# Full-height low parts in the scores of 64-wide heads

## The chip, the cores and the metric

The kernel runs on one core of a Trainium2 chip. The time is the device time of one execution in microseconds (us). The core's engines are named as in the profile: PE (TensorE; PEld is its loading of weights, the stationary operand), DVE (VectorE), ACT (ScalarE), POOL (GpSimd) and SP (SyncE, which here issues the DMAs, in order). Data lie in on-chip memory in 128 partitions; PE multiplies over the partitions, its rows, and accumulates into PSUM.

## What is computed

The reference takes 512 tokens of width 1024 through a gMLP layer, an attention layer with forget gates (FoX) and, in a second block, an mLSTM beside a sparse attention. Each of the first two layers has a SwiGLU FFN. The parts that the change touches are three kinds of score, each a product over heads that are 64 wide:

```python
# FoX, 16 heads of 64
logits = einsum('bhqd,bhkd->bhqk', qi, k) * scale
logits = logits + di[..., :, None] - dcum[..., None, :]
p = softmax(where(kpos <= qpos, logits, -inf))
# indexer of the second block, 8 heads of 64, one key for all heads
sc = relu(einsum('bthd,bsd->bths', iqb, ik))      # then weighted, summed over heads, 128 best keys kept
# sparse attention of the second block, 8 heads of 64: the same scores with a relative bias and the kept keys
```

All is float32. The kernel splits an operand into a high part, rounded to the format that PE multiplies fast, and the low part, the rest, and sums the products of the parts.

## The kernel before

**Large products.** Weights come by SP in chunks of 512 KB (`load_w`, line 271), ACT rounds them to high parts (line 279), DVE or POOL subtracts for the low parts (line 282), and PE runs three matmuls for each pair of tiles (`mm3`, lines 416 to 418): high by high, high by low, low by high, all over 128 rows with 512 columns.

**Scores of 64-wide heads.** A head fills only half of the rows. Therefore `stack` (line 911) lays the queries of a head out over all 128 partitions: the high part on one half, the low part on the other. The keys' high part lies on both halves (`spread`, line 919, does this on the way to DRAM and back), so that one matmul over 128 rows gives high by high and low by high. The third product, queries' high by keys' low, is a second matmul over the 64 rows that hold the queries' high part. It adds to the same PSUM tile:

```python
PE.matmul(sp[:, o:o + w], qs_[:, qs], kh[:, 0:w], start=True, stop=False)        # line 974
PE.matmul(sp[:, o:o + w], qs_[me, qs], kl[me, 0:w], start=False, stop=True)      # line 975
```

`me` is the upper or lower half of the partitions, by the head's number in its pair. The keys' low parts of both heads of a pair share one tile `kl`, a half each. The indexer does the same (lines 1289 and 1290) with one key for all heads, whose high and low parts both lie on both halves already.

**The attentions.** `attention` (line 952) runs over heads. The four tiles of 128 queries are taken in the order SO = (2, 0, 3, 1); tile i has (i + 1) x 128 keys, at least 256 columns. DVE adds the bias and takes the maximum from PSUM (line 980), ACT takes the exponential (982); then come the normalisation, PE's transposes (1001), their splitting by ACT and DVE (1004, 1005) and the product with the values (1016). The scores of a head go ahead of the transposes and values of the head before. Steps of other large products stand between them (`between`, line 507; FILL says how many at which place), so that PE has work while the softmax runs. FoX runs this twice, for 8 heads each, from about 835 to 1000 us; the second block once, from 1567 to 1655 us. The order within each engine is set by a planner that works from the written order and its own costs, but for two stretches that this change doesn't touch.

**The keys' way.** `kdone` (line 1061) splits the keys of a pair of heads and writes them to DRAM, `loader` (line 926) reads the tiles of a pair back while the pair before is worked on. For FoX a pair has three tiles, out of NKB = 6 buffers which the raw keys use before them (`ka`, line 1058). For the second block `ev_a` (line 1265) writes five tiles a pair, two stacks of queries and three of keys, and NQK = 9 buffers hold what is read back. The writes and reads are on SP's queue with all other loads: between the second group of keys and the next product stand, for instance, the eight loads of the layer's input (line 1112), which ACT and DVE turn into `hx` (lines 1113 to 1115).

**The indexer.** Lines 1282 to 1299 go over query tiles 1 to 3 and 8 heads: a pair of matmuls, ACT's relu (1292), DVE's weighted sum (1297). Then DVE searches the 128 best keys (1322, 1323), while PE works on the products that follow.

Of the kernel before, what the change touches and what calls it, by code (L numbers as in the profile page):

```python
"""One-core Trainium2 kernel: a gMLP layer, a FoX attention layer (each with a SwiGLU FFN), then an
mLSTM + indexer-sparse-attention block with a per-layer-embedding gate, for 512 tokens of width 1024.

Large products run as three float32r passes over exactly split operands (hi*hi + hi*lo + lo*hi).
"""
# [30 lines left out]
NKB = 6  # L36
NZ = 26
NQK = 9
# [22 lines left out]
# ------------------------------------------------------------------ host layout  # L61
def _wa(w):
    """[K, N] -> [N/128, 128 (k in tile), K/128 * 128]: stationary chunks of 128 outputs."""
    k, n = w.shape
    return np.ascontiguousarray(
        w.reshape(k // P, P, n // P, P).transpose(2, 1, 0, 3).reshape(n // P, P, (k // P) * P))


def _wb(w):
    """[K, N] -> [N/512, K/256, 128, 2 * 512]: moving chunks of two k tiles by 512 outputs."""  # L70
    k, n = w.shape
    return np.ascontiguousarray(
        w.reshape(k // 256, 2, P, n // 512, 512).transpose(3, 0, 2, 1, 4).reshape(n // 512, k // 256, P, 1024))
# [26 lines left out]
def layout(i):  # L100
# [33 lines left out]
    # gMLP  # L134
# [14 lines left out]
    # FoX  # L149
# [8 lines left out]
    # second block  # L158
# [3 lines left out]
    # rows of the last tile: keys 0-63, input gates 64-67, forget gates 96-99, indexer weights 100-107  # L162
# [28 lines left out]
# ------------------------------------------------------------------ kernel body  # L191
def body(tc, nc, a):
    V, S_, G, PE = nc.vector, nc.scalar, nc.gpsimd, nc.tensor

    with ExitStack() as es:
# [55 lines left out]
        # ---------------- constants  # L251
# [14 lines left out]
        # ---------------- weights: load, split  # L266
# [7 lines left out]
        def wsplit(src, n=1024, share=0, alloc=None, raw=None):  # L274
            """share: every share-th low part on GpSimd"""
# [9 lines left out]
        # ---------------- modulation vectors, worked off between weight chunks  # L285
# [21 lines left out]
        def fill(n=1):  # L307
            """one column's load, and the product for the one loaded before"""
# [25 lines left out]
        def gain(csc, gname):  # L334
            """gain * (1 + scale), a column per feature tile"""
# [5 lines left out]
        def gb_row(cg, gname):  # L341
            """gate * gain, on every partition"""
# [13 lines left out]
        # ---------------- norms, transposes  # L356
        def rsq(out, ss, scale):
            """out = 1 / sqrt(ss * scale + eps)"""
# [3 lines left out]
        def norm_rows(xr, out):  # L362
            """out = xr / rms(xr), a token tile in two halves"""
# [8 lines left out]
        def to_T(ts, xn, g, sh, hi, lo, js=range(KD), spill=None):  # L372
            """token-major halves of the tiles ts -> feature-major hi, lo; what is transposed goes
            to spill as well"""
# [39 lines left out]
        # ---------------- products  # L414
# [5 lines left out]
        def gemm_a(h, w, n, evac, m=P, group=0, nfill=0, share=0, gshare=1):  # L420
            """out^T tile i (m outputs by 512 tokens), weights stationary. The first group goes by
            halves of the tokens, since the second half of h comes later."""
# [20 lines left out]
        def gemm_b(h, w, groups, kt, evac, head=False, tail=0, nfill=0, share=0, raws=(), hshare=1):  # L443
            """out tile (g, t): 128 tokens by 512 outputs, activations stationary. The last chunks
            of a group (all of them in the first with head) go token tile by token tile."""
# [25 lines left out]
        def chunks_a(h, w, n, evac):  # L471
            """gemm_a's weight chunks for between(): source, number of steps, step"""
# [15 lines left out]
        def chunks_b(h, w, g, kt, evac):  # L488
            """gemm_b's weight chunks of a group for between()"""
# [17 lines left out]
        def between(chunks, share=1):  # L507
            """products to be placed between the steps of something else: a function that emits the
            next n steps (all that are left without n)"""
# [24 lines left out]
        def post(gb, xsrc, xdst, alloc, done):  # L534
            """x += gate * rms_norm(y), then x / rms(x) by token tiles"""
# [23 lines left out]
        def halves(h, g, sh, spill=None):  # L559
            """takes normalised token tiles; transposes two at a time"""  # L560
# [33 lines left out]
        # ================= layer 0: gMLP  # L594
# [5 lines left out]
        with tc.tile_pool(name="l0", bufs=20) as p0:  # L600
# [8 lines left out]
            # loads in the order of their use: per-layer embedding, x, modulation with weights  # L609
# [16 lines left out]
            # relative bias by distance 511 - m  # L626
# [26 lines left out]
            def norm2(t):  # L653
                """two token tiles"""
# [14 lines left out]
            with tc.manual_schedule(engines={mybir.EngineType.Activation, mybir.EngineType.DVE, mybir.EngineType.PE, mybir.EngineType.SP}):  # L669
                S_.activation(crow, crow, AF.Silu)  # L670
                # brings in the table of the square root
# [31 lines left out]
                # the first products start as the modulation of each feature tile is there  # L703
# [50 lines left out]
                # both gains and the scale of the attention's scores, for the keys  # L754
# [40 lines left out]
            def ready(g):  # L795
                """the spatial weights of a group of features, and its values normalised"""
# [46 lines left out]
        # ================= FFN 0  # L843
# [10 lines left out]
        # ================= layer 1: FoX attention  # L854
        cmask = const("cmask", [P, P], "mask")
        def headnorm(out, alloc, done=None):
            """rms norm of heads of 64, token-major; one square root for a group of token tiles"""
# [21 lines left out]
        def vsplit(g, t, pt, alloc, done):  # L879
            """values of 8 heads -> tiles of 4 heads; a pair of heads as hi lo lo hi"""  # L880
# [9 lines left out]
        def logsig(out, xin, n, tmpa):  # L890
            """min(x, 0) - ln(1 + exp(-|x|))"""
# [13 lines left out]
        def pt_tiles(pool, bufs=1):  # L905
            """transposed probabilities, hi and lo: the blocks of key tile s from PTO[s] on"""
# [4 lines left out]
        def stack(src, alloc):  # L911
            """two heads, feature-major: hi over lo for the first, lo over hi for the second"""
# [6 lines left out]
        def spread(d, q0, hi, lo):  # L919
            """two heads' keys to DRAM: hi of each on both halves of the partitions, and their lo"""  # L920
# [131 lines left out]
        with tc.tile_pool(name="x", bufs=1) as px:  # L1052
# [116 lines left out]
            def fprep(pr):  # L1169
                return *stack(pair_t(qt_, pr), qk), *kload(pr)  # L1170
# [446 lines left out]
```

## Time and profile before

| what | value |
|---|---|
| median of 3 runs | 1938.3 us (1936.7, 1938.3, 1945.61) |
| the profiled execution | 1936.7 us, with a span of 1936.7 us |
| PE busy | 1880.1 us, 97% of the span |
| weight loads (PEld), beside PE | 1523.1 us |
| DVE, ACT, POOL busy | 1123.1, 794.6, 375.8 us |
| chain that ended last | PE 78%, DVE 11%, DMA 7% |

A busy PE isn't a PE at its peak: matmuls overlap, and each counts from its start to its modelled end. How fast PE really goes is read from the starts of successive matmuls in the order of time. The granted clock is a share: 1.00 is 2.4 GHz, 0.50 is 1.2 GHz. Idle time of an engine other than the slowest costs nothing by itself; it matters who waits for that engine.

### The profile page before, as it was taken

What the parts mean: (1) busy time and instruction counts of PE and PEld (TensorE: products, weight loads), DVE (VectorE), ACT (ScalarE), POOL (GpSimd) and SP (SyncE); (2) the same over time, 40 slices, a digit from 0 to 9 for tenths busy, and PEclk for the clock granted to TensorE, in tenths of its full rate; (3) what the DMA queues carried; (4) which work ended last, traced back from release to release, by engine and by line L of the source; (5) the groups of instructions that cost most, each with busy time, mean ns of one, the idle gap of its engine ahead of it and who ended that gap; (6) DMA issues with size and microseconds to landing.
All of it is one profiled execution on the core that took longest, in us unless ns stands there. A gap on an engine that the chain in (4) does not pass through costs nothing.

```text
span 1936.7 us, 23791 instructions
## 1 busy us (share of the span) xinstructions
PE 1880.1 (97%) x8688; PEld 1523.1 (79%) x8688; DVE 1123.1 (58%) x2132; ACT 794.6 (41%) x1395; POOL 375.8 (19%) x216
## 2 busy tenths in 40 slices
PE   7999998999999999999998999999989999999998
PEld 5788877888878877877777888888876877888887
DVE  7879735677762275367757333322365967856534
ACT  5334324422231255477655222222344246455334
POOL 2100123222220013433322111100020353022011
PEclk9999999999999999999998999999987999999999
DMA  8674753477763446733512322233243633322522
GB/s 330 235 274 137 251 194 109 147 265 260 260 219 109 141 138 205 247 120 126 172 67 97 112 94 96 98 109 126 103 136 98 187 129 111 115 93 88 191 96 100
DMA packets 106191, 299.46 MB, mean 155 GB/s; under 512 B 11893, under 2 KB 14749, under 8 KB 106074
## 3 DMA queue, kind: packets, MB, share of 16 engines
q1 hardware_dynamic: 106074, 297.94, 45.3%
q8 instruction: 69, 1.13, 0.2%
q14 instruction: 48, 0.39, 0.1%
HBM read 266.35 MB, written 34.16 MB: 155 GB/s over the span
## 4 chain that ended last, share of the span: by engine, by line
PE 78%; DVE 11%; DMA 7%; issue 2%; ACT 2%; POOL 0%; SPq 0%; DVEq 0%; ACTq 0%
PE acc L416 22%; PE acc L418 22%; PE acc L417 22%; DMA raw<-in_ada 6%; DVE raw L302 3%; PE tp L975 2%; PE tp L1016 2%; DVE d L302 1%; PE tp L1001 1%; PE tp L974 1%; DVE h L408 1%; PE tp L384 1%; DVE wlo L282 1%; DVE h L409 1%; PE tp L815 1%
## 5 line engine op out<-in xcount | busy, mean ns | idle before, releaser
L279 ACT ACTIVATE whi<-raw 128x1024 fp32r<-128x1024 f32 x293 | 309.9, 1059 | 679.4 <-PE acc L418 305.5
L282 POOL TENSOR_TENSOR wlo<-raw,whi 128x1024 fp32r<-128x1024 f32 x124 | 305.1, 2464 | 1368.3 <-ACT whi L279 1189.1
L417 PE MATMUL acc<-h,whi 128*128 128x512 f32 (+1 forms) x1112 | 418.2, 376 | 10.5 <-DVE h L409 10.4
L416 PE MATMUL acc<-h,whi 128*128 128x512 f32 (+1 forms) x1112 | 418.6, 376 | 5.5 <-DVE h L408 5.2
L418 PE MATMUL acc<-h,wlo 128*128 128x512 f32 (+1 forms) x1112 | 417.5, 375 | 3.3 <-DVE wlo L282 2.7
L282 DVE TENSOR_TENSOR wlo<-raw,whi 128x1024 fp32r<-128x1024 f32 x169 | 212.4, 1259 | 312.6 <-ACT whi L279 312.2
L417 PEld LDWEIGHTS acc<-h,whi 128*128 128x128 f32 x1112 | 212.5, 191 | 48.6 <-DVE h L409 12.7
L416 PE MATMUL acc<-whi,h 128*128 128x512 f32 x608 | 242.5, 399 | 7.9 <-DVE h L408 6.5
L416 PEld LDWEIGHTS acc<-h,whi 128*128 128x128 f32 x1112 | 212.8, 191 | 43.2 <-DVE h L408 6.0
L418 PEld LDWEIGHTS acc<-h,wlo 128*128 128x128 f32 x1112 | 212.7, 191 | 41.9 <-DVE wlo L282 4.5
L417 PE MATMUL acc<-wlo,h 128*128 128x512 f32 x608 | 240.0, 395 | 3.2 <-DVE wlo L282 3.2
L418 PE MATMUL acc<-whi,h 128*128 128x512 f32 x608 | 240.8, 397 | 0.0
L302 DVE SCALAR_TENSOR_TENSOR raw<-raw,cact 128x1024 f32<-128x1024 f32 x96 | 148.9, 1562 | 75.4 <-DMA raw<-in_ada 69.8
L416 PE MATMUL acc<-whi,s 128*128 128x512 f32 (+1 forms) x488 | 190.4, 390 | 0.7 <-DVE t L1308 0.7
L417 PE MATMUL acc<-wlo,s 128*128 128x512 f32 (+1 forms) x488 | 190.7, 391 | 0.0
L418 PE MATMUL acc<-whi,s 128*128 128x512 f32 (+1 forms) x488 | 190.2, 390 | 0.0
L416 PEld LDWEIGHTS acc<-whi,h 128*128 128x128 f32 x608 | 115.5, 190 | 34.2 <-DVE h L408 7.6
L417 PEld LDWEIGHTS acc<-wlo,h 128*128 128x128 f32 x608 | 115.2, 189 | 27.0 <-DVE wlo L282 4.1
L418 PEld LDWEIGHTS acc<-whi,h 128*128 128x128 f32 x608 | 115.2, 189 | 26.5 <-DVE h L409 2.4
L416 PEld LDWEIGHTS acc<-whi,s 128*128 128x128 f32 x488 | 91.7, 188 | 20.1 <-DVE t L1308 1.1
L417 PEld LDWEIGHTS acc<-wlo,s 128*128 128x128 f32 x488 | 91.7, 188 | 18.8
L418 PEld LDWEIGHTS acc<-whi,s 128*128 128x128 f32 x488 | 91.7, 188 | 18.6
(349 smaller groups left out, 2416.4 us busy)
## 6 DMA issues: line engine op xcount, KB each, us to landing
raw<-in_ada SPq DMA_DIRECT2D x96, 512.0 KB, 4.3
raw<-in_w_gu SPq DMA_DIRECT2D x88, 512.0 KB, 3.5
raw<-in_w_dn SPq DMA_DIRECT2D x44, 512.0 KB, 3.2
scr<-t SPq DMA_DIRECT2D x60, 256.0 KB, 4.1
raw<-in_w_o SPq DMA_DIRECT2D x20, 512.0 KB, 3.4
row<-scr SPq DMA_DIRECT2D x36, 256.0 KB, 3.4
d<-in_ada SPq DMA_DIRECT2D x16, 512.0 KB, 6.9
raw<-in_w_v SPq DMA_DIRECT2D x16, 512.0 KB, 5.2
```

Source lines behind the costliest of these rows:

```text
L279: S_.activation(hi[:, 0:n], raw[:, 0:n], AF.Copy)
L282: e.tensor_sub(lo[:, 0:n], raw[:, 0:n], hi[:, 0:n].bitcast(F32))
L302: V.scalar_tensor_tensor(raw, raw, 1.0, cact[0], ALU.mult, ALU.mult, accum_out=modc[:, col:col + 1])
L384: PE.transpose(src[:, i * P:(i + 1) * P], xn[t][j // 4][:, (j % 4) * P:(j % 4 + 1) * P], ident[:])
L408: V.tensor_copy(hi[j][:, c], fj)
L409: V.tensor_sub(lo[j][:, c], fj, hi[j][:, c].bitcast(F32))
L416: PE.matmul(out, lh, rh, start=start, stop=False)
L417: PE.matmul(out, lh, rl, start=False, stop=False)
L418: PE.matmul(out, ll, rh, start=False, stop=stop)
L815: PE.matmul(sp[:, n * P:(n + 1) * P], vt[n, i // 4][:, o], rows[i // 4][:, o], start=True, stop=True)
L975: PE.matmul(sp[:, o:o + w], qs_[me, qs], kl[me, 0:w], start=False, stop=True)
L1016: PE.matmul(po[:, s * P:512], vd[s, hd // 4][:, hq * P:(hq + 1) * P], pt[:, PTO[s]:PTO[s] + n], start=(q == 0 and s == 0), stop=(q == 1 an ...
```

## The change

The keys' low parts get the layout of their high parts: each head's low part lies on both halves of the partitions. The second matmul then runs over all 128 rows, as the first does, and adds the product of both low parts to what was computed before. A pair of heads so has four key tiles instead of three, in DRAM and on chip; the buffers are NKB = 8 and NQK = 10. The indexer's key needs no new layout, and only its second matmul changes. Comments and docstrings are taken out too.

```diff
-NKB = 6
+NKB = 8
-NQK = 9
+NQK = 10
...
-        def spread(d, q0, hi, lo):
-            for q, half in enumerate((TOP, BOT)):
-                nc.sync.dma_start(d[q0 + q].rearrange("(a p) n -> p a n", a=2),
-                                  hi[half].unsqueeze(1).broadcast_to((64, 2, 512)))
-            nc.sync.dma_start(d[q0 + 2], lo)
+        def spread(d, at, hi, lo):
+            for q, (src, half) in zip(at, ((hi, TOP), (lo, TOP), (hi, BOT), (lo, BOT))):
+                nc.sync.dma_start(d[q].rearrange("(a p) n -> p a n", a=2),
+                                  src[half].unsqueeze(1).broadcast_to((64, 2, 512)))
...
-                q0, q1, k0, k1, kl = qk[pr]
-                qs_, kh = ((q0, k0), (q1, k1))[hv]
-                me = slice(64 * hv, 64 * hv + 64)
+                qs_, kh, kl = qk[pr][hv]
...
                     PE.matmul(sp[:, o:o + w], qs_[:, qs], kh[:, 0:w], start=True, stop=False)
-                    PE.matmul(sp[:, o:o + w], qs_[me, qs], kl[me, 0:w], start=False, stop=True)
+                    PE.matmul(sp[:, o:o + w], qs_[:, qs], kl[:, 0:w], start=False, stop=True)
...
-            kscr, vscr = scratch([8, 3, P, 512]), scratch([8, P, 512])
+            kscr, vscr = scratch([8, 4, P, 512]), scratch([8, P, 512])
...
-                    spread(kscr[pr], 0, hi.bitcast(F32), lo.bitcast(F32))
-            kload = loader(lambda dt: tile_of(px, "k", dt, bufs=NKB), kscr, 3, 8)
+                    spread(kscr[pr], range(4), hi.bitcast(F32), lo.bitcast(F32))
+            kload = loader(lambda dt: tile_of(px, "k", dt, bufs=NKB), kscr, 4, 8)
...
-                return *stack(pair_t(qt_, pr), qk), *kload(pr)
+                q, k = stack(pair_t(qt_, pr), qk), kload(pr)
+                return (q[0], *k[0:2]), (q[1], *k[2:4])
...
-            ascr = scratch([4, 5, P, 512])
+            ascr = scratch([4, 6, P, 512])
...
-                        nc.sync.dma_start(d[q, half], hi[half])
-                        nc.sync.dma_start(d[q, ot], lo[half])
+                        nc.sync.dma_start(d[3 * q, half], hi[half])
+                        nc.sync.dma_start(d[3 * q, ot], lo[half])
                 else:
-                    spread(d, 2, hi, lo)
+                    spread(d, (1, 2, 4, 5), hi, lo)
...
-                    rws = slice((hd % 2) * 64, (hd % 2) * 64 + 64)
...
-                    PE.matmul(sp[:, 0:n], qs_[rws, qs], ikl[rws, 0:n], start=False, stop=True)
+                    PE.matmul(sp[:, 0:n], qs_[:, qs], ikl[:, 0:n], start=False, stop=True)
...
-            attention(range(8), loader(qk2, ascr, 5, 4), av, md_dsa, None, lambda: pt_tiles(pz, 2), oa2,
+            qkload = loader(qk2, ascr, 6, 4)
+            def aprep(pr):
+                t = qkload(pr)
+                return t[0:3], t[3:6]
+            attention(range(8), aprep, av, md_dsa, None, lambda: pt_tiles(pz, 2), oa2,
```

## Rows read from the trace of the kernel before

**Rows 1.** Stretch; its length; PE, PEld, DVE, ACT, POOL busy (xcount); granted clock; DMA; GB/s.
```profile
830.00:1010.00 180.00, 179.88 (x854) 134.46 (x853) 131.14 (x452) 126.86 (x283) 59.56 (x31) 1.00 0.37 123
1495.00:1560.00 65.00, 64.91 (x286) 53.31 (x286) 64.31 (x179) 18.39 (x27) 21.42 (x11) 1.00 0.57 174
1560.00:1665.00 105.00, 104.59 (x469) 79.17 (x468) 68.75 (x179) 56.76 (x127) 41.09 (x35) 0.97 0.39 127
```

**Rows 2.** The chain of waits from 830 to 1010 us, shares by line.
```profile
by line: PE acc L416 18.2%; PE acc L418 18.0%; PE acc L417 17.8%; PE tp L975 12.4%; PE tp L1016 11.6%; PE tp L1001 10.2%; PE tp L974 8.3%; PE tp L944 1.7%; ACT q L982 0.7%; DVE q L991 0.7%; DVE pt L1005 0.3%; DVE sm L987 0.1%; issue 0.1%; P
```

**Rows 3.** PE in time in FoX: start us, duration us, line, tiles, shape, count.
```profile
862.53 0.28 PE L974 MATMUL tp<-k,qk 128*128 128x256 f32 x1
...
863.05 0.45 PE L1016 MATMUL tp<-pt,v 128*128 128x256 f32 x2
863.34 0.44 PE L974 MATMUL tp<-k,qk 128*128 128x512 f32 x1
...
864.13 0.50 PE L417 MATMUL acc<-wlo,hm 128*128 128x512 f32 x1
864.47 0.28 PE L974 MATMUL tp<-k,qk 128*128 128x256 f32 x1
...
868.95 1.39 PE L1016 MATMUL tp<-pt,v 128*128 128x512 f32 x8
870.18 0.45 PE L416 MATMUL acc<-whi,hm 128*128 128x512 f32 x1
...
871.62 0.33 PE L974 MATMUL tp<-k,qk 128*128 128x384 f32 x1
871.88 0.43 PE L975 MATMUL tp<-k,qk 64*128 64x384 f32 x1
872.25 0.38 PE L974 MATMUL tp<-k,qk 128*128 128x256 f32 x1
...
872.87 0.50 PE L974 MATMUL tp<-k,qk 128*128 128x512 f32 x1
...
873.73 0.50 PE L416 MATMUL acc<-whi,hm 128*128 128x512 f32 x1
```

**Rows 4.** Weight loads in the same stretch; in brackets the idle time before one.
```profile
863.71 0.18 PEld L975 LDWEIGHTS tp<-k,qk 64*128 64x128 f32 x1 [0.24 <-issue]
...
867.13 0.19 PEld L417 LDWEIGHTS acc<-wlo,hm 128*128 128x128 f32 x1
```

**Rows 5.** PE in time in the indexer, where its stages begin and end.
```profile
1459.54 0.35 PE L1289 MATMUL tp<-s,s 128*128 128x256 f32 x1
...
1469.86 0.34 PE L1289 MATMUL tp<-s,s 128*128 128x384 f32 x1
...
1477.88 0.79 PE L1289 MATMUL tp<-s,s 128*128 128x512 f32 x1
...
1489.46 0.79 PE L418 MATMUL acc<-h,wlo 128*128 128x512 f32 x1
```

**Rows 6.** ACT and DVE in time in the indexer's last query tile.
```profile
1480.88 0.60 ACT L1292 ACTIVATE t<-tp 128x512 f32<-128x512 f32 x1 [0.85 <-PE tp L1290]
1481.51 1.28 DVE L1297 SCALAR_TENSOR_TENSOR s<-t,iw,s 128x512 f32<-128x512 f32 x2 [0.43 <-ACT t L1292]
```

**Rows 7.** Busy time by engine, as rows 1, in two stretches at half clock.
```profile
1472.38:1492.86 20.48, 20.48 (x34) 9.83 (x34) 8.06 (x16) 7.41 (x14) 0.00 (x0) 0.50 0.13 49
1571.37:1578.19 6.82, 6.82 (x18) 4.42 (x18) 4.27 (x19) 3.65 (x11) 1.67 (x1) 0.50 0.62 205
```

**Rows 8.** SP's queue in time: the loads of the next layer's input.
```profile
777.30 4.01 SPq L1112 DMA_DIRECT2D t<-scr  x8
```

**Rows 9.** Line 922, writes of the keys' high parts: ns min, median, max.
```profile
L922 SPq DMA_DIRECT2D scr<-t x24: 581/614/1973, 739.0 to 1522.9; - x24
```

**Rows 10.** Busy time by engine, as rows 1, around the loads of rows 8.
```profile
775.00:790.00 15.00, 15.00 (x68) 12.43 (x67) 7.21 (x21) 9.78 (x17) 4.79 (x2) 1.00 0.93 315
```

**Rows 11.** The chain of waits behind these loads: start us, us, what.
```profile
783.33 0.82 ACT t L1113
```

## The prediction, made before the changed kernel ran

> **What bounds the kernel now.** I read the busy times by stage first. In the FoX attention PE is busy for 179.88 of 180 us, DVE for 131.14 and ACT for 126.86; in the second block's attention PE has 104.59 of 105 us and DVE 68.75 [rows 1]. The chain of waits over the FoX stretch says the same by line: nearly all of it is PE, and 12.4% + 8.3% of it are the two score matmuls, lines 975 and 974 [rows 2]. So in both attentions a microsecond less on PE is a microsecond less of the whole, until DVE or ACT becomes the slowest.
>
> Then I read the order in time on PE. In the fence of rows 3 the difference between one row's start and the next row's start is the step, what a matmul really costs the stream (its own duration is longer, since matmuls overlap). Eight 128-row matmuls of line 1016, twice 512 + 384 + 256 + 128 columns, take 870.18 - 868.95 = 1.23 us for 2560 columns, 0.48 ns a column [rows 3]. So a 128-row matmul of 256, 384 or 512 columns steps by 0.123, 0.184 or 0.246 us, and a pair of them by 0.246, 0.369 or 0.492. A score pair (128 rows, then 64) steps by much more: with 256 columns 863.05 - 862.53 = 0.52 and 872.87 - 872.25 = 0.62, mean 0.57; with 384 columns 872.25 - 871.62 = 0.63; with 512 columns 864.13 - 863.34 = 0.79 and 873.73 - 872.87 = 0.86, mean 0.825 [rows 3]. In the 384 pair the 128-row half takes 0.26 and the 64-row half 0.37, so both sides of the change in shape are slow. The weight loads show where the time goes: line 975's load of 64 rows begins only when its own matmul does, at 863.71, with 0.24 us idle ahead of it, while a 128-row load after a 128-row matmul (867.13) begins as the matmul before it starts, and is hidden [rows 4].
>
> The Trainium skill gives this behaviour a name: "TensorEngine Tiling (Array Packing)", Tiling Modes, Key Properties, says that changing the tiling mode drains the TensorE. The pair's steps here agree with it (0.63 against 0.369 us for 384 columns), and by that rule all of the excess goes when both matmuls have 128 rows. Against it stands "TensorE: Matmul & The Clock Gate", The mechanism: weight loads overlap matmuls in flight only where their row groups differ. By that rule two 128-row matmuls, which share every row group, could not hide a load either, and the pair would cost what it costs now. The load at 867.13 contradicts it; it is the second rival below.
>
> **The change part by part.**
>
> Score pairs, warm clock. A head has four query tiles, of 256, 256, 384 and 512 columns (the loop over SO, with at least 256). FoX has 16 heads: 32 pairs of 256 save 0.57 - 0.246 = 0.324 each (10.4 us), 16 of 384 save 0.26 (4.2), 16 of 512 save 0.33 (5.3): 19.9 us. The second block has 8 heads of the same tiles: 10.0 us. Bounds for one pair from single rows: 0.27 to 0.37 us.
>
> The matmul behind a pair. After a 64-row matmul the next 128-row load isn't hidden yet: line 417 at 864.13 steps by 0.34 instead of 0.246 [rows 3]. Other pairs are followed by the next pair, whose steps are counted already. From 862 to 876 us four of seven pairs are followed by such a step; if that holds for all 96 pairs, 55 give 0.09 each: 5.0 us (0 to 9).
>
> The indexer (lines 1289, 1290). From the first pair at 1459.54 to the first with 384 columns at 1469.86 are 10.3 us; from there to the first with 512 at 1477.88 are 8.0, and to the end of the pairs at 1489.46 are 11.6, 1.45 us a pair [rows 5]. Here the drained stream is slow and the clock is at its lower level too: granted 0.50 of full speed, 1.2 GHz, from 1472.38 to 1492.86, behind a stretch of score pairs [rows 7]. For the last two query tiles, 19.6 us, PE alone would need 8 x (0.369 + 0.492) = 6.9 us at full clock. ACT takes 0.60 a head with 512 columns and DVE 1.28 / 2 = 0.64 [rows 6]; 16 x 0.64 = 10.2 us if PE had to keep pace with DVE. PE can run some heads ahead of both (four PSUM tiles, nine t tiles), so I take 8.5, between the two: 11.1 us saved. The first tile's stretch holds 8 pairs (2.0 us new) and eleven other 512 matmuls (2.7 us) beside a few tiny ones; at full clock 5 of 10.3 us would do, and I take 4 us saved, since the clock there also dips after an idle stretch that stays. The matmuls from 1489.46 to 1492.86 still run at the lower level: half of 3.4 us, 1.7. Together 16.8 us. If the clock stays low anyway, the pairs of the last two tiles need twice 0.861, 13.8 us, and about 6 are saved; with PE unhindered 19.6.
>
> The clock in the second attention. From 1571.37 to 1578.19 it is at half too, right behind its first two heads' pairs [rows 7]; half of 6.8 is 3.4, of which the pairs inside are counted already: 2 us (0 to 3.4).
>
> Sum of what goes: 19.9 + 10.0 + 5.0 + 16.8 + 2 = 53.7 us.
>
> What the other engines give back. FoX would shrink from 180 to about 155 us, and DVE with 131 us and ACT with 127 would then be busy for 84% and 82% of it. No engine is over its limit, but both are served in order, and the scores of one head, its softmax and the transposes of the head before hang together; the trace of before doesn't show such waits, since PE hides them. Ends: nothing, and 15 us (most of what FoX gains). I take 5, nearer to nothing as the shares are under 90%. The second attention, with DVE at 69 of about 92 us, gives back 2 (0 to 7).
>
> After the indexer DVE has the search for the best keys, busy for 64.31 of the 65 us from 1495 [rows 1], beside PE's 64.91. Both start as the indexer lets them: DVE's split of a weight chunk waits for PE to use up an older one. So both move ahead together, and I cost this at nothing. If DVE fell behind, the second attention's first scores would wait for its masks; the cover is small, 2 us of that are in the 2 above.
>
> More DMAs. Each pair of heads writes four key tiles instead of three, and loads one more: 8 + 4 pairs. Issuing costs SP 0.61 us for such a write [rows 9] and 4.01 / 8 = 0.50 for such a load [rows 8]. They matter in one place: the second group of keys' writes stand on SP ahead of the eight loads of the next layer's input (line 1112, from 777.30), in a stretch in which the DMA engines are 93% busy [rows 8, 10]. Four more writes push these loads back by 4 x 0.61 = 2.4 us. Their first consumer (ACT, line 1113, 783.33) is on the chain that PE waits for [rows 11]; about 1.5 us of it is covered by the loads being early. I take 2 us (-1 to 4; below nothing, since NKB 8 lets all raw key tiles stand at once). In both attentions SP's loads are issued about a head's time ahead, and PE waited for none; 1 us (0 to 4) for the second block's writes beside weight loads. The larger NKB and NQK hold two pairs of FoX keys as before, and 10 of 12 tiles of the second block against 9 of 10, so two tiles instead of one wait for the head before; the load ahead hides it.
>
> Given back: 5 + 2 + 2 + 1 = 10 us. Net 43.7. The profiled execution took 1936.7 us, which is its span and the lowest of the three runs; 1936.7 - 43.7 = 1893.0. The median of the runs is 1.6 us higher, and with it 1894.6: I say 1894.
>
> **Rivals.** *The next engine binds.* DVE and ACT give back 15 us in FoX and 7 in the second attention, and the indexer runs at the lower clock level and saves 6 instead of 16.8: 53.7 - 10.8 - 25 = 18 us, so 1919 to 1920. For it: 73% and 70% busy now, in-order queues, and DVE saturated behind the indexer. Against: DVE idles now largely until PE's scores come.
>
> *The shape isn't the price* (slower). If the second matmul is slow because a load for the same row groups can't be hidden, or because it accumulates on the first, 128 rows cost what 64 do: no term of the sum comes, and only DMAs are added. At least 2.4 us at line 1112; at most, if all of SP's extra issues lay on the path, 12 x (0.61 + 0.50) = 13.3 us: 1941 to 1952. It decides from the point at which a 128-row pair of 384 columns still steps by 0.63. Against it: the other products also accumulate into one PSUM tile, and their steps are 0.48 ns a column.
>
> *The change does less than it says*: only the half behind the 64-row matmul gets quicker, while the scores' first half stays. In the 384 pair that is (0.37 - 0.184) of 0.261, 70% of the gain, and 0.7 x 53.7 - 10 = 28 us: 1911. Against it: 0.26 for a 128-row matmul that steps by 0.184 elsewhere.
>
> **How the numbers follow.** Forecast 0.74, the partial gain 0.08, the next engine 0.12, the shape not the price 0.06. The range 1877 to 1915 reaches from all of the sum with almost nothing given back (57.9 saved, 1880, and 3 us for the spread of a pair's step) past the partial gain to near the next-engine case; less than 2 in 10 lie outside. About 0.5%, 10 us, is what a measurement can tell from no change. Faster by more: 0.92; within: 0.04 (part of the last two cases); slower: 0.04.
>
> **What would show it.** Steps of lines 974 and 975 near 0.12, 0.18 and 0.25 us; no idle ahead of line 975's weight load; the granted clock at full between 1470 and 1490; FoX's stretch about 20 us shorter, the second attention's about 11. Wrong if the steps stay at 0.3 and more, or if PE's idle time in the attentions grows by over 20 us with DVE or ACT as the releaser.

## The result, and the profile after

| | median us | runs | ratio to before | 95% interval |
|---|---|---|---|---|
| before | 1939.11 | 4 (1936.7 to 1945.61) | | |
| changed kernel | 1914.87 | 4 (1910.77 to 1920.14) | 0.9865 | 0.9839 to 0.9892 |

The change makes the kernel faster by 0.0135 x 1939.1 = 26 us (21 to 31); the two medians lie 24.2 apart. Forecast were 43.7. The direction and the mechanism held; some 18 us of the gain are missing, 16 by the two profiled executions. The profiled execution of the changed kernel took 1910.77 us, with a span of 1908.9, 27.8 less than the span before. Its page begins so (engine, busy us, share of the span, number of instructions):

```profile
span 1908.9 us, 23835 instructions
PE 1832.5 (96%) x8688; PEld 1514.8 (79%) x8688; DVE 1130.9 (59%) x2132; ACT 792.2 (41%) x1395; POOL 375.9 (20%) x216
```

PE has as many matmuls as before and is busy 47.6 us less, but the span fell by 27.8 only: PE also idles more. To see where, I numbered PE's matmuls from 0 in order of time in each trace and compared the start of the n-th, since each kernel has 8688 of them. The table gives start minus start before; the last two columns are experiments told below, e6 and e8. At the 3000th matmul (681 us), ahead of every edit, the profiled executions of all runs told here lie from 2.8 us earlier to 10.7 us later than before; therefore stages are compared, and not whole executions.

| matmul | before, us | changed | e6, POOL queue | e8, half loads | what lies ahead of it |
|---|---|---|---|---|---|
| 3300th | 751.4 | -1.7 | +0.4 | +2.4 | first layer; spread between executions |
| 3600th | 820.8 | +13.8 | +4.9 | +2.5 | the stage that writes the keys |
| 4650th | 1048.2 | +0.7 | -9.7 | -11.9 | FoX |
| 6600th | 1462.7 | -0.4 | -11.2 | -13.1 | FFN, products of the second block, first indexer pairs |
| 6750th | 1513.0 | -18.3 | -29.1 | -31.0 | indexer |
| 7350th | 1650.0 | -27.9 | -39.1 | -41.0 | second attention |
| last | 1928.9 | -27.8 | -39.0 | -41.3 | end |

So three stages gained: FoX 13.8 - 0.7 = 13.1, the indexer 17.9 and the second attention 9.6 us. One stage, between 751 and 821 us, lost 15.5 us, more than all of FoX's gain.

**The pairs.** PE in time in FoX of the changed kernel (start us, duration us, line, tiles, shape; lines 971 and 972 are the two score matmuls), to be laid beside [rows 3]:

```profile
864.93 0.28 PE L971 MATMUL tp<-k,qk 128*128 128x256 f32 x1
865.05 0.28 PE L972 MATMUL tp<-k,qk 128*128 128x256 f32 x1
865.17 0.40 PE L418 MATMUL acc<-whi,hm 128*128 128x512 f32 x1
865.40 0.40 PE L416 MATMUL acc<-whi,hm 128*128 128x512 f32 x1
...
866.56 0.39 PE L971 MATMUL tp<-k,qk 128*128 128x512 f32 x1
866.78 0.39 PE L972 MATMUL tp<-k,qk 128*128 128x512 f32 x1
867.01 0.39 PE L418 MATMUL acc<-whi,hm 128*128 128x512 f32 x1
...
869.89 0.35 PE L971 MATMUL tp<-k,qk 128*128 128x384 f32 x1
870.08 0.34 PE L972 MATMUL tp<-k,qk 128*128 128x384 f32 x1
870.25 0.40 PE L417 MATMUL acc<-wlo,hm 128*128 128x512 f32 x1
```

A pair with 256, 384 and 512 columns steps by 0.24, 0.36 and 0.45 us here (the median of FoX's sixteen pairs with 512 columns is 0.49), where [rows 3] gave 0.57, 0.63 and 0.825. A matmul of line 418 behind a pair steps by 0.23 us (865.17 to 865.40), where line 417 took 0.34 in [rows 3]. The weight load of the second half begins with the first half's matmul, with no idle time ahead of it, unlike in [rows 4]:

```profile
866.56 0.19 PEld L972 LDWEIGHTS tp<-k,qk 128*128 128x128 f32 x1
```

**The indexer.** PE in time, the first pair, the first of 384 and of 512 columns, and the end, as in [rows 5]:

```profile
1460.51 0.36 PE L1286 MATMUL tp<-s,s 128*128 128x256 f32 x1
...
1466.27 0.34 PE L1286 MATMUL tp<-s,s 128*128 128x384 f32 x1
...
1469.08 0.39 PE L1286 MATMUL tp<-s,s 128*128 128x512 f32 x1
...
1472.82 0.40 PE L418 MATMUL acc<-h,wlo 128*128 128x512 f32 x1
```

That is 12.3 us instead of 29.9, and the last two tiles take 6.55 instead of 19.6. The busy times by stretch show the rest (stretch; length; PE, PEld, DVE, ACT and POOL busy with the number of instructions; granted clock; DMA share; GB/s). The last two rows are the stage that lost time:

```profile
835.00:990.00 155.00, 149.89 (x796) 121.50 (x794) 128.48 (x438) 119.87 (x270) 57.46 (x30) 1.00 0.46 150
1459.00:1473.00 14.00, 13.02 (x72) 11.19 (x72) 13.46 (x27) 12.02 (x28) 0.00 (x0) 1.00 0.62 153
...
775.00:790.00 15.00, 3.60 (x16) 2.63 (x15) 6.19 (x12) 6.39 (x9) 0.00 (x0) 0.69 0.94 314
780.80:797.90 17.10, 5.60 (x12) 3.97 (x13) 13.29 (x19) 10.83 (x14) 7.04 (x3) 0.50 0.82 290
```

The clock is granted in full through the indexer. In FoX PE is now idle for 5.1 of 155 us, and before for 0.1 of 169 us with the same 796 matmuls:

```profile
821.30:990.22 168.92, 168.80 (x796) 125.00 (x794) 124.17 (x439) 120.84 (x271) 57.20 (x30) 1.00 0.39 128
```

The longest of PE's waits from 832 to 1000 us of the changed kernel is for DVE, and so are nearly all others there (who waits <- for whom: us in total, times, longest):

```profile
PE tp L943 <- DVE sm L977: 1.5, 1, 1.5
```

These waits cost more than the 5.1 us that the profile counts as idle, since idle time counts from a matmul's modelled end, 0.40 us behind its start, and the next could start after 0.23. I summed the steps of these matmuls in both traces. FoX's 64 pairs took 41.3 us before, and at the median steps of the changed kernel they need 20.9, so 20.5 less. The 31 matmuls of lines 416 to 418 behind a pair go from 0.34 to 0.23 us each, 3.3 less. That makes 24, and the stretch got only 13.7 us shorter (168.9 to 155.2): the other engines take back some 10 us, an estimate from these sums.

In the 15 us around the loads of [rows 8], where PE was full before [rows 10], PE is busy for 3.60 us with the same DMA share (0.94, and 0.93 before).

**What PE waited for.** PE's longest wait of the changed kernel from 720 to 830 us:

```profile
PE acc L416 <- ACT whi L279: 12.2, 1, 12.2
```

It is new, 12.2 us once. The order in time of ACT and PE there says for what:

```profile
789.67 1.06 ACT L279 ACTIVATE whi<-raw 128x1024 fp32r<-128x1024 f32 x1 [0.24 <-DMA raw<-in_w_vv]
790.78 1.22 PE L416 MATMUL acc<-whi,h 128*128 128x512 f32 x2 [12.18 <-ACT whi L279]
```

PE waits for the rounding of a weight chunk, and ACT for that chunk's load. Why the load is late stands on SP's queue of the changed kernel (start, us, line, tiles, number of DMAs issued):

```profile
730.45 3.65 SPq L271 DMA_DIRECT2D raw<-in_w_vv  x3
737.29 41.27 SPq L922 DMA_DIRECT2D scr<-t  x32
...
779.30 4.18 SPq L1109 DMA_DIRECT2D t<-scr  x8
783.52 10.30 SPq L271 DMA_DIRECT2D raw<-in_w_vv  x5
```

All 32 key writes (8 pairs of heads, 4 tiles each) stand in one block, and the last five weight chunks behind them. In the kernel before, the writes came in two groups, with four of these chunks between them:

```profile
739.02 2.04 SPq L922 DMA_DIRECT2D scr<-t  x2
...
750.44 10.95 SPq L271 DMA_DIRECT2D raw<-in_w_vv  x4
...
764.90 1.24 SPq L922 DMA_DIRECT2D scr<-t  x2
```

The block isn't 41 us of issuing: 32 writes with a median of 0.67 us are some 21. SP waits in it for the keys of the second group, which ACT and DVE split only from 762 us on (SP's largest wait from 730 to 800 us, in the changed kernel; line 1065 is ACT's part of the split keys):

```profile
SPq L922 <- ACT t L1065: 13.8, 2, 10.1
```

For those 10 us nothing behind the write can go out, and the DMA engines run dry. The stretch from 756 to 763 us in the changed kernel, DMA share 0.00:

```profile
756.00:763.00 7.00, 5.25 (x32) 3.66 (x31) 5.97 (x9) 2.51 (x5) 2.36 (x1) 1.00 0.00 0
```

and in the kernel before, where the chunks used that time and SP's longest wait of this kind was 3.7 us:

```profile
756.00:763.00 7.00, 5.25 (x28) 3.13 (x27) 5.34 (x7) 2.90 (x6) 2.37 (x1) 1.00 0.37 121
```

The same chunks were asked for at 750.44 before and at 783.52 now. PE had used up what it had by 778.6 and stood until 790.78. Meanwhile the granted clock fell to 0.50, from 780.80 to 797.90, so that PE worked at 1.2 GHz for 7 us more when it could work again. 12.2 us of waiting and half of those 7 account for the 15.5 us that this stage lost.

### The profile page after: what moved, and what is told of

It reads as the page before. It is cut to its first block, busy times and chain, and to the rows that moved or that the text cites. A ratio compares the mean times of both kernels' runs of the same rounds, so it can differ in the third digit from the quotient of the medians.

```text
span 1908.9 us, 23835 instructions
## 1 busy us (share of the span) xinstructions
PE 1832.5 (96%) x8688; PEld 1514.8 (79%) x8688; DVE 1130.9 (59%) x2132; ACT 792.2 (41%) x1395; POOL 375.9 (20%) x216
## 5 line engine op out<-in xcount | busy, mean ns | idle before, releaser
L416 PE MATMUL acc<-whi,h 128*128 128x512 f32 x608 | 241.4, 398 | 19.5 <-ACT whi L279 12.2
```

Source lines behind the costliest of these rows:

```text
L416: PE.matmul(out, lh, rh, start=start, stop=False)
```

## The experiments

The question: is the missing gain the price of the key writes in that stage (SP's queue and the idle PE behind it), or do the other engines hold FoX and the indexer back?

### The indexer alone

The kernel before, with the indexer's second matmul over 128 rows and nothing else changed; its key lies on both halves already, so no DMA is added.

```diff
-PE.matmul(sp[:, 0:n], qs_[rws, qs], ikl[rws, 0:n], start=False, stop=True)
+PE.matmul(sp[:, 0:n], qs_[:, qs], ikl[:, 0:n], start=False, stop=True)
```

> The kernel before with one line changed: the indexer's second matmul runs over 128 rows; both attentions stay as they were. If the shape of the second matmul is the price, the indexer's 24 pairs step by 0.12, 0.18 and 0.24 us for each half, the granted clock stays at 1.00 between 1465 and 1490, and the whole is 17 to 19 us faster: about 1920. If instead most of what the second block gained comes from its attention, it is under 12 us faster.

Measured: 1925.09 against 1946.82 us, 0.9900 (0.9867 to 0.9934), so 19.5 us faster. In the stretch that was at half clock in [rows 7] the clock is full (columns as for the stretches above):

```profile
1465.00:1490.00 25.00, 24.02 (x121) 20.02 (x120) 23.41 (x40) 16.55 (x33) 0.00 (x0) 1.00 0.60 171
```

One line gives three quarters of what the whole change gives. The indexer isn't where the gain is missing.

### The writes alone

The kernel before with one more write for each pair of heads, of the same size and kind as the changed kernel's fourth. Nothing reads it, and the scores are as before.

```diff
-kscr, vscr = scratch([8, 3, P, 512]), scratch([8, P, 512])
+kscr, vscr = scratch([8, 4, P, 512]), scratch([8, P, 512])
...
+nc.sync.dma_start(kscr[pr, 3].rearrange("(a p) n -> p a n", a=2),
+                  lo.bitcast(F32)[TOP].unsqueeze(1).broadcast_to((64, 2, 512)))
```

> The kernel before with one more write of 256 KB for each of the 8 pairs of FoX keys, which nobody reads; all matmuls as before. Theory 1, the order on SP's queue: the planner now puts four of the eight value-weight loads behind all of the 32 writes; PE runs out of weights between 770 and 800 and the whole is 8 to 17 us slower. Theory 2, bytes: 2 MB more at the 315 GB/s that the stretch reached are 6.7 us at most, spread over two places, so 0 to 7 us slower. Theory 3, that FoX's gain is eaten by DVE and ACT in the softmax: no difference here.

Measured: 1956.44 against 1946.82 us, 1.0063 (1.0039 to 1.0088), so 12 us slower (8 to 17). SP's queue again has the weight chunks behind all writes and the layer's input:

```profile
791.50 2.62 SPq L271 DMA_DIRECT2D raw<-in_w_vv  x4
```

SP's largest wait from 730 to 800 us is again the one for the second group's keys:

```profile
SPq L922 <- ACT t L1068: 13.5, 2, 9.8
```

and so is PE's from 720 to 830 us that for the chunk:

```profile
PE acc L416 <- ACT whi L279: 8.0, 1, 8.0
```

The clock is at half from 794.8 to 808.5 us. So eight extra writes cost this stage 12 us with FoX's scores untouched. This run doesn't say by itself whether the order or the added bytes do it: both changed.

### The second block alone

The changed kernel with FoX's part undone: three key tiles, NKB = 6, and the second matmul of FoX's scores over 64 rows again.

```diff
-NKB = 8
+NKB = 6
...
-kscr, vscr = scratch([8, 4, P, 512]), scratch([8, P, 512])
+kscr, vscr = scratch([8, 3, P, 512]), scratch([8, P, 512])
...
-return (q[0], *k[0:2]), (q[1], *k[2:4])
+return tuple((q[h][64 * h:64 * h + 64], k[2][64 * h:64 * h + 64], q[h], k[h]) for h in range(2))
```

> The changed kernel with FoX as before (three key tiles a pair, 64-row second matmuls, 6 buffers); indexer and second attention changed. Theory 1 (the stage of the keys' writes takes what FoX gains): 28 us faster than the kernel before, so 1910 to 1912, as fast as the whole change within 4 us, since FoX's half nets to about nothing. Theory 3 (FoX gains nothing because its softmax engines bind): also about 28 us, but then the stretch before 830 us differs by nothing between this kernel and the whole change.

Measured: 1916.86 against 1946.82 us, 0.9862 (0.9825 to 0.9899), so 27 us faster: as much as the whole change, within the intervals. FoX's part nets to nothing within these intervals (by the table, 13.1 gained and 15.5 lost). In this kernel's trace the start of the n-th matmul is +2.4 us against before at the 3300th and at the 3600th alike: the stage of the writes lost nothing. That FoX gains in the attention and loses it ahead of it is seen in both directions.

### The indexer's matmuls in groups

The kernel before, with 64-row second matmuls kept, but written as four first matmuls and then four second ones. It asks whether the 64-row matmul is slow or the change of height.

```diff
...
+if hd % 4 == 0:
+    for h_ in range(hd, hd + 4):
+        sps[h_] = tp()
+        PE.matmul(sps[h_][:, 0:n], iq[h_ // 2][h_ % 2][:, qs], ikh[:, 0:n], start=True, stop=False)
+    for h_ in range(hd, hd + 4):
+        rws = slice((h_ % 2) * 64, (h_ % 2) * 64 + 64)
+        PE.matmul(sps[h_][:, 0:n], iq[h_ // 2][h_ % 2][rws, qs], ikl[rws, 0:n], start=False, stop=True)
```

> The kernel before with the indexer's matmuls in groups of four heads: four first matmuls over 128 rows, then the four second ones over 64, as far as the planner keeps them together; their number and rows are as before. If the price is paid at each change between 128 and 64 rows, matmuls that follow one of their own height step by 0.12, 0.18 and 0.24 us, only those at a change are slow, and the whole is 6 to 14 us faster. If a 64-row matmul is slow in itself, its steps stay at 0.31 us and more wherever it stands, and the time stays within 3 us.

Measured: 1936.6 against 1946.82 us, 0.9957 (0.9937 to 0.9978), so 8.4 us faster. The planner kept the groups in part only, and the two patterns stand beside each other in PE's order of time (the matmul of 1480.91, then two more of its kind, in a row):

```profile
1480.17 0.44 PE L1293 MATMUL tp<-s,s 64*128 64x384 f32 x1
1480.54 0.44 PE L1290 MATMUL tp<-s,s 128*128 128x384 f32 x1
1480.91 0.44 PE L1293 MATMUL tp<-s,s 64*128 64x384 f32 x1
1480.92 0.61 PE L1293 MATMUL tp<-s,s 64*128 64x384 f32 x2
1481.45 0.44 PE L1290 MATMUL tp<-s,s 128*128 128x384 f32 x1
```

Alone between 128-row matmuls, a 64-row one steps by 0.37 us (1480.17 to 1480.54), and so does the 128-row one behind it. Three in a row take 0.54 (1480.91 to 1481.45), but not evenly: the first two start 0.003 us apart (neighbouring heads lie on different halves of the partitions), the third at 1481.19, 0.28 behind them, and the 128-row matmul 0.26 behind the third. So a 64-row matmul isn't slow in itself, as two of them side by side take 0.28; what is slow is a 64-row and a 128-row matmul in turn. "TensorEngine Tiling (Array Packing)" of the Trainium skill, Tiling Modes, Key Properties, says that a change of the tiling mode drains the engine. This trace agrees. For matmuls in turn the price is the trace's own, about 0.19 us for each change at 384 columns: the step of 0.37 less 0.18, the full speed of [rows 3]. The half clock stays in part, from 1484.5 to 1498.2 us, so this version gets less than the first experiment; changes of height stay in part, too.

### The low parts' writes on another queue

The changed kernel with the low parts' writes issued from ACT instead of SP, and, in a second kernel, from POOL (`nc.gpsimd`). The bytes are the changed kernel's; SP's own part is half as long.

```diff
-nc.sync.dma_start(d[q].rearrange("(a p) n -> p a n", a=2),
+(nc.sync if src is hi else nc.scalar).dma_start(d[q].rearrange("(a p) n -> p a n", a=2),
```

> The changed kernel, but the two writes of low parts of each pair (FoX and second block) are issued from ACT's queue instead of SP's: the same four writes and bytes. The planner then has the value-weight loads between the writes on SP again. Theory 1 (order on SP): PE's wait of 12 us and the half clock near 780 go, 12 to 18 us faster than the changed kernel, so 1897 to 1903, less some us if ACT's issuing delays its own work. Theory 2 (bytes): the traffic is the same, so within 4 us of the changed kernel, 1915.

Measured from ACT: 1916.08 against 1940.86 us, 0.9864 (0.9843 to 0.9886), 26 us faster. That is what the changed kernel gives, so the gain that the first theory asked for didn't come. The weight chunks are back between the two groups of writes, yet PE waits elsewhere: counted as in the table, the stage from 751 to 821 us loses 14.2 us, nearly as much as in the changed kernel. ACT now holds up its own work while the writes are issued, for instance (ACT in time, in brackets the idle time ahead):

```profile
756.61 0.69 ACT L1065 ACTIVATE t<-tp,kgain 128x512 fp32r<-128x512 f32 x1 [8.29 <-DMA scr<-t]
```

PE's largest wait from 700 to 860 us is one that has 1.0 us in all in the kernel with the second block alone:

```profile
PE acc L416 <- DVE v L887: 4.5, 2, 4.2
```

By itself this run decides nothing between order and bytes, because the remedy had a price of its own. It does show that chunks between the groups aren't enough for the gain.

> As the run with ACT's queue, but from POOL's. Theory 1: 12 to 18 us faster than the changed kernel, 1897 to 1903, if POOL, which also makes low parts of weights there, isn't held up. Theory 2: 1915, as the changed kernel.

Measured from POOL: 1905.0 against 1940.86 us, 0.9815 (0.9793 to 0.9837), 36 us faster. SP's queue of this kernel has the chunks between the groups:

```profile
739.43 13.40 SPq L922 DMA_DIRECT2D scr<-t  x8
752.93 2.88 SPq L271 DMA_DIRECT2D raw<-in_w_vv  x3
...
765.31 11.40 SPq L922 DMA_DIRECT2D scr<-t  x8
```

Expected were 1897 to 1903. The gain is 10 us more than the 26 of the changed kernel, and 6 more than the 30 of its repeat below. SP's longest wait for keys is 3.7 us, as before the change. PE's wait for whi is gone, and its longest wait from 700 to 832 us is another, on DVE's splitting of the values (line 887):

```profile
PE acc L416 <- DVE v L887: 3.6, 2, 3.4
```

In order of time these steps stand among those that make `hx` (lines 1110 to 1112), and ACT's first of these waited for its load, one of the eight of line 1109, which SP issued from 778.95 us on:

```profile
783.69 0.82 ACT L1110 ACTIVATE t<-t,modc,gcol 128x512 f32<-128x512 f32 x1 [1.84 <-DMA t<-scr]
```

With all of the added bytes still written, the stage loses 4.9 - 0.4 = 4.5 us by the table instead of 15.5. So some 11 us of the loss go with SP standing in front of the chunks, and up to 4.5 with the added transfers or with POOL's issuing, which this run doesn't separate.

### Two writes, and loads that read rows twice

The changed kernel with plain writes (high parts, low parts: two for a pair) and loads that read a half's 64 rows twice, with a step of zero between the two readings.

```diff
-for q, (src, half) in zip(at, ((hi, TOP), (lo, TOP), (hi, BOT), (lo, BOT))):
-    nc.sync.dma_start(d[q].rearrange("(a p) n -> p a n", a=2),
-                      src[half].unsqueeze(1).broadcast_to((64, 2, 512)))
+for q, src in zip(at, (hi, lo)):
+    nc.sync.dma_start(d[q], src)
...
+return bass.AP(b.tensor, b.offset, [[0, 2], [512, 64], [1, 512]])
```

> The changed kernel with two plain writes a pair (high parts, low parts) instead of four; each load of a key tile reads its half of the rows twice, so that the tiles on chip are the same. Theory 1: with 16 writes ahead instead of 32 the value-weight loads are back between the groups; 15 to 18 us faster than the changed kernel, 1896 to 1900, faster than both kernels. Theory 2 (bytes): also faster, by about 7 us at most (4 MB fewer written). If the read of a half twice is slow, the loads land later than 4 us and PE waits for keys in the attentions.

Measured: 1993.94 against 1940.86 us, 1.0274 (1.025 to 1.0298), 53 us slower. There are fewer writes than ever, but the loads block SP. Its queue in FoX:

```profile
871.06 9.79 SPq L933 DMA_DIRECT2D k<-scr  x3
880.95 4.96 SPq L241 DMA_DIRECT2D row<-scr  x1
```

Three such loads take 9.8 us to issue (4.01 for eight in [rows 8]), and a load right behind them takes 5. It isn't issuing alone: while they stand there, the DMA engines are busy for 0.13 of the time and move 50 GB/s, where [rows 10] have 0.93 and 315:

```profile
876.00:881.00 5.00, 5.00 (x27) 4.29 (x27) 4.01 (x9) 4.04 (x8) 2.41 (x2) 1.00 0.13 50
```

In these loads the two readings are the outermost step of the pattern. The writes of `spread` read rows twice too, by a step of zero further in, and take some 0.6 us [rows 9]; so the repetition alone isn't what is slow. PE's largest waits from 700 to 1010 us:

```profile
PE tp L970 <- DVE sm L976: 25.2, 4, 14.4
PE acc L416 <- DVE v L887: 24.2, 1, 24.2
```

### Three writes, and the low parts loaded in halves

The changed kernel with the three old writes a pair; each low tile is filled by two plain loads of 64 rows, one into each half. No write is added, and SP gets two more loads a pair than the changed kernel.

```diff
-for q, (src, half) in zip(at, ((hi, TOP), (lo, TOP), (hi, BOT), (lo, BOT))):
+for q, half in zip(at, (TOP, BOT)):
     nc.sync.dma_start(d[q].rearrange("(a p) n -> p a n", a=2),
-                      src[half].unsqueeze(1).broadcast_to((64, 2, 512)))
+                      hi[half].unsqueeze(1).broadcast_to((64, 2, 512)))
+nc.sync.dma_start(d[at[2]], lo)
...
+for o in (TOP, BOT):
+    nc.sync.dma_start(t[o], src[0][p_, i, half])
```

> The changed kernel with the three writes a pair of the kernel before (the low parts written once, as they are); each low tile is loaded by two plain loads of 64 rows, so a pair of FoX heads has six loads instead of four. On chip all is as in the changed kernel. Theory 1 (the fourth write puts the value-weight loads behind all key writes on SP): the planner has SP's order of the kernel before again, the stage from 715 to 835 us costs what it did before, and the FoX gain of 14 to 19 us stays: 40 to 46 us faster than the kernel before, about 1896 on a chip where that takes 1939. If the loads of 64 rows are slow to issue as those were that read a half twice (about 5 us each), PE waits for keys and rows in the attentions, and it is slower than the changed kernel.

Measured: 1900.17 (5 runs, 1897.2 to 1905.47) against 1946.22 us, 0.9773 (0.9748 to 0.9797), 44 us faster (39 to 49). It beats both kernels. On SP's queue the chunks stand between the groups, and its longest wait for keys is 3.7 us:

```profile
753.29 10.53 SPq L271 DMA_DIRECT2D raw<-in_w_vv  x4
...
767.34 1.24 SPq L922 DMA_DIRECT2D scr<-t  x2
```

PE and the clock are full where the changed kernel stood still, with the DMA engines at 0.95, so a busy DMA isn't what stops PE:

```profile
775.00:790.00 15.00, 15.00 (x68) 12.43 (x67) 7.21 (x16) 7.39 (x13) 6.95 (x3) 1.00 0.95 322
```

### The changed kernel beside it

The changed kernel once more, unedited, on the same chip as the one with half loads.

> The changed kernel itself, beside the one with loads of halves on one chip: 23 to 31 us faster than the kernel before, and 12 to 20 us slower than the kernel with loads of halves by theory 1; equal to it within 4 us if the stage's loss comes from anything else than its writes.

Measured: 1915.58 against 1946.22 us, 0.9846 (0.9824 to 0.9869), 30 us faster, and 15.4 us above the version with half loads. The stall is not chance: this execution too has one wait of 12.2 us of line 416 for line 279 and a half clock of 17.1 us (786.4 to 803.5).

## Why the prediction was right in kind and wrong in size

**The steps of the pairs: right.** Forecast were 0.246, 0.369 and 0.492 us, measured 0.24, 0.36 and 0.45. The change of height was all of the excess, the load of 128 rows hides, and the rival that the shape isn't the price falls: its point of decision, 0.63 us for 384 columns, reads 0.36. The load at 866.56 shares all rows with the matmul that it hides behind. "TensorE: Matmul & The Clock Gate" of the Trainium skill, The mechanism, has the sentence that weight loads overlap matmuls in flight only where their row groups differ; taken by itself it doesn't hold for this kernel. The partial-gain rival falls too: both halves got quicker.

**FoX: its net 4 to 5 us too high.** Pairs 19.9, two thirds of the 5.0 for matmuls behind them (64 of 96 pairs) and 5 given back make 18.2. Measured are 13.1, and 14.4 in the version with half loads. What goes was sized rightly: 20.5 for pairs and 3.3 for the matmuls behind them, by the steps summed above. The term that failed is "What the other engines give back": it took 5 us, nearer to nothing because DVE and ACT would be busy for under 90% of the stretch, and some 10 were given back. DVE is busy for 128.48 of the 155 us, 83%, and PE still waits for it, some 15 times.

**The indexer and its clock: right.** 16.8 forecast, 17.9 (the trace) and 19.5 (the first experiment, 13 to 26) measured. PE ran ahead of DVE through the last two tiles: 6.55 us, where 8.5 was taken and PE alone was reckoned at 6.9.

**The second attention: 2 us too high.** 10.0 for pairs, 1.7 for matmuls behind them and 2 for the clock, less 2 given back, are 11.7; measured 9.6. The clock is still at half there for 3.4 us (1555.6 to 1559.0), where it was for 6.8. From 1530 to 1640 us PE has a wait of 2.1 us for DVE's line 988, where the kernel with the indexer alone has only one of 0.4 us in its second attention.

**The step that failed most: "More DMAs".** It said: "Four more writes push these loads back by 4 x 0.61 = 2.4 us", and took 2 us (-1 to 4) for the stage. Measured are 15.5 us. The step took the order on SP as given and added the issue time of four writes. But that order is planned from the program, and with eight writes more the second group came ahead of the last weight chunks. The loads that came late were other ones than the text named: line 1112's (1109 after) moved from 777.30 to 779.30, about as the step says, and the chunks of line 271 from 750.44 to 783.52. And what held them up wasn't the issuing, but one write that waited 10 us for its data in front of them. The text had no term for that, nor for the clock that falls while PE stands. By the two profiled executions the forecast is missed by 43.7 - 27.8 = 15.9 us: 13.5 from this step, 5.1 from FoX and 2.1 from the second attention, against 1.1 that the indexer gave more, the 1 us for other writes that didn't come, and 2.8 between these stages, of which 1.7 lie ahead of the 3300th matmul; up to rounding.

**The rival that the next engine binds** gave 1919, close to the median, and happened in part: of its 15 us in FoX some 10 came. But its indexer at the lower clock ran at the full one, and the largest loss was in a stage that it doesn't name. A time near a rival's number is no evidence for the rival.

**Luck.** The measured median, 1914.87, is 0.13 us inside the range of 1877 to 1915. The range reached so far for the partial-gain rival, which fell, and the next-engine rival, and not for a stall ahead of FoX. That it holds the time is luck.

**What stays open.** Why the plan tips with the fourth write wasn't found, and the order was never changed with all else the same. That the order is the cause rests on SP's wait and the dry DMA engines in the traces, and on two versions with the chunks between the groups: from POOL, with the same bytes, 4.5 us are lost; with half loads and fewer bytes, none. Against it stands the version from ACT, with chunks between the groups and 14.2 us lost, which is put down to its own waits; that is argued and not shown.

## What to carry to other kernels

Where matmuls of 64 and 128 rows alternate, filling the shorter operand to full height can be free on TensorE; grouping by height got 8.4 of 19.5 us in the indexer. Read the step between starts, not the duration, and open rows that stand for several matmuls. A DVE that was busy for 83% of a stretch still held up PE there, so a share under 90% is no reason to price the waits near nothing. An added DMA is priced by the queue's new order: find what waits behind it while it waits for its own data, and how long PE can go without that. Where the layout can be made by plain loads, as here by two half loads, compare that with making it by writes in a busy stretch.

## What the runs showed of the hardware that was not expected

- A load that reads the same 64 rows twice, by a step of zero as the outermost one, took up to 5.7 us to issue (9.79 us for three, at 50 GB/s), and the next DMA on the queue 5, while two plain loads of 64 rows into the two halves stood in the queue for about 0.5 us each.
- PE standing for 12.2 us cost more than these 12.2: the granted clock was at 0.50 for 17.1 us, of which 7.1 lay behind the wait.
- Of three 64-row matmuls of 384 columns in a row, the first two started 0.003 us apart and the third 0.28 us behind them; alone between 128-row ones each took a step of 0.37.
